# Second parts of the weights: a subtraction on GpSimd, or a DMA that adds the weights from DRAM

## The chip, the cores and the metric

The kernel runs on one core of one Trainium2 chip. A core has five engines that run side by side: TensorE (PE in the profile, with its weight loads as PEld), VectorE (DVE), ScalarE (ACT), GpSimd (POOL) and SyncE (SP, which here only issues DMAs). They work on tiles in SBUF; PE writes to PSUM banks. Sixteen DMA engines move data between DRAM and SBUF, for whichever engine issues the DMA. The metric is the device time of one execution in microseconds (us), the median of several runs.

## What is computed

Two transformer-like blocks in float32 over one sequence of 512 tokens of width 1024. Cut to what matters here:

```python
x = layer_norm(x)
h = x @ w_in + b_in                                    # heads of two attentions
mix = concat(swa_sink_attention(h), dsa_attention(h)) @ w_o + b_o
x = layer_norm(ALPHA * x + mix)
x = layer_norm(ALPHA * x + memory_cross_attention(x))  # xa_wq, xa_wk, xa_wv, xa_wo
x = layer_norm(ALPHA * x + square(relu(x @ w_up + b_up)) @ w_down + b_down)
h = x + ssd_mixer(rms_norm(x))                         # ssm_in, chunked scan, ssm_out
h = h + mla_mixer(rms_norm(h))                         # mla_in, latent attention, mla_out
return rms_norm(h)
```

Nearly all of the arithmetic is in the products with the weight matrices.

## The kernel before

Every product is made of three matmuls in the type float32r, which keeps fewer bits than float32. Each float32 operand is split in a first part H (its value rounded to float32r) and a second part L (what the rounding left over), and `mm3` (lines 127 to 131) adds H·H, L·H and H·L into one PSUM bank: a line for each, L129, L130 and L131.

`wload` (L115) does this for the weights. It loads a tile of up to 128 x 1024 float32 (512 KB) with a DMA from SP into `wraw` (3 buffers), ScalarE copies it into `wh` (5 buffers, L121), which rounds it, and GpSimd subtracts `wh` from `wraw` in pieces of 512 columns into `wl` (5 buffers, L124). There are 254 such tiles in the program. For eight of them, those of `xa_wk` at the start, the caller names the engine (`leng`): VectorE for the first, GpSimd for the others. For the other 246 `leng` is None and GpSimd is taken.

The matrix products that use `wload` are written in a few forms. `gemm_s` takes one tile for each 128 output columns and runs 24 matmuls of 512 columns with it (eight slices times three). `gemm_m` takes two slices of 512 columns of a tile for each group of tokens (w_down, xa_wv). `gemm_q` (w_o, xa_wo, ssm_out, mla_out) takes two or four tiles together and goes through the tokens with them, with matmuls of 256 columns; its last group always has four tiles and is gone through four times, once for each 128 tokens. The tile framework orders the instructions of each engine beforehand by its own estimate of when each could run, so the order that stands in the program on one engine depends on what the others are given. Each engine then executes its own list in order and waits at a semaphore where it must. A buffer of `wh` or `wl` is written anew when PE is done with its last matmul, one of `wraw` when both readers are done.

GpSimd also has other work in its list: the products with 1/den in the softmax (L653, L798, L878), the sums and gates of the state space mixer (L1015, L1018, L1055, L1066, L1067, and L95 for a power), and splits of a few activations (L146, L153).

Of the kernel before, what the change touches and what calls it, by code (L numbers as in the profile page):

```python
# [10 lines left out]
ALU = mybir.AluOpType  # L11
# [9 lines left out]
def f32(ap):  # L21
    return ap.bitcast(F32)


class Net:
# [89 lines left out]
    def wload(self, ap, n=1024, shape=None, leng=None):  # L115
        nc = self.nc
        raw = self.wp.tile([P, 1024], F32, tag="wraw", name=self.nm("wraw"), bufs=3)
        h = self.wp.tile([P, 1024], F32R, tag="wh", name=self.nm("wh"), bufs=5)
        l = self.wp.tile([P, 1024], F32R, tag="wl", name=self.nm("wl"), bufs=5)
        nc.sync.dma_start(raw[:, :n], ap)  # L120
        nc.scalar.activation(h[:, :n], raw[:, :n], AF.Copy)  # L121
        for o in range(0, n, 512):
            e = slice(o, min(n, o + 512))
            (leng or nc.gpsimd).tensor_tensor(l[:, e], raw[:, e], f32(h[:, e]), op=ALU.subtract)  # L124
        return h, l

    def mm3(self, out, aH, aL, bH, bL, first, last):
# [1496 lines left out]
```

## Time and profile before

| | us |
|---|---|
| median of 3 runs (1727.59 to 1733.44) | 1730.55 |
| profiled execution, its own time | 1732.23 |
| span of the profile | 1730.5 |
| PE busy | 1663.9 (96%) |
| DVE busy | 927.3 (54%) |
| POOL busy | 907.9 (52%) |
| ACT busy | 834.1 (48%) |

Busy time is the time in which an instruction of that engine ran; shares are of the span. The rest of the execution's own time (1.7 us) lies outside the span. A wait is put down to the instruction whose semaphore ended it. Matmuls overlap in PE, so a matmul's duration is longer than the distance to the next, and a PE that is shown as busy may still have small gaps.

### The profile page before, as it was taken

What the parts mean: (1) busy time and instruction counts of PE and PEld (TensorE: products, weight loads), DVE (VectorE), ACT (ScalarE), POOL (GpSimd) and SP (SyncE); (2) the same over time, 40 slices, a digit from 0 to 9 for tenths busy, and PEclk for the clock granted to TensorE, in tenths of its full rate; (3) what the DMA queues carried; (4) which work ended last, traced back from release to release, by engine and by line L of the source; (5) the groups of instructions that cost most, each with busy time, mean ns of one, the idle gap of its engine ahead of it and who ended that gap; (6) DMA issues with size and microseconds to landing.
All of it is one profiled execution on the core that took longest, in us unless ns stands there. A gap on an engine that the chain in (4) does not pass through costs nothing.

```text
span 1730.5 us, 27236 instructions
## 1 busy us (share of the span) xinstructions
PE 1663.9 (96%) x10203; PEld 1479.8 (86%) x10203; DVE 927.3 (54%) x1981; ACT 834.1 (48%) x1694; POOL 907.9 (52%) x833
## 2 busy tenths in 40 slices
PE   6999999999999999999999899998999999999998
PEld 6877889889988888887978788888999888989898
DVE  7579763742653014303778877779321306667522
ACT  4455663453443123313557767767433326565532
POOL 6746434353375445544558777777634544344431
PEclk9999999999999999999999999999999999999999
DMA  7634313232232222222332222332324332122341
GB/s 282 196 107 130 106 48 143 95 110 86 86 120 87 97 99 88 95 98 95 125 117 92 86 86 98 110 101 95 146 98 155 130 123 76 52 75 92 110 141 50
DMA packets 68181, 187.23 MB, mean 108 GB/s; under 512 B 9968, under 2 KB 16544, under 8 KB 67792
## 3 DMA queue, kind: packets, MB, share of 16 engines
q1 hardware_dynamic: 50128, 152.95, 26.0%
q10 hardware_dynamic: 17632, 30.43, 5.5%
q8 instruction: 80, 1.31, 0.3%
q0 software_dynamic: 288, 2.10, 0.3%
q14 instruction: 53, 0.43, 0.1%
HBM read 163.86 MB, written 14.78 MB: 103 GB/s over the span
## 4 chain that ended last, share of the span: by engine, by line
PE 71%; DVE 14%; ACT 5%; issue 4%; DMA 3%; POOL 3%; ACTq 0%; DVEq 0%; SPq 0%; POOLq 0%
PE mm L129 12%; PE mm L131 12%; PE mm L130 12%; PE acc L129 5%; PE acc L130 5%; PE acc L131 5%; PE sc L130 2%; PE sc L131 2%; PE sc L129 2%; DMA Dm<-acd 2%; DVE xbc L948 2%; POOL wl L124 2%; PE pv L130 2%; PE pv L131 1%; PE pv L129 1%
## 5 line engine op out<-in xcount | busy, mean ns | idle before, releaser
L124 POOL TENSOR_TENSOR wl<-wraw,wh 128x512 fp32r<-128x512 f32 (+1 forms) x498 | 665.3, 1360 | 515.5 <-ACT wh L121 492.7
L121 ACT ACTIVATE wh<-wraw 128x1024 fp32r<-128x1024 f32 (+4 forms) x254 | 258.3, 1019 | 404.0 <-PE acc L131 123.7
L129 PE MATMUL mm<-xaH,wh 128*128 128x512 f32 x552 | 221.3, 401 | 1.8 <-DVE qbL L140 1.1
L131 PE MATMUL mm<-xaH,wl 128*128 128x512 f32 x552 | 220.8, 400 | 0.0
L130 PE MATMUL mm<-xaL,wh 128*128 128x512 f32 x552 | 220.5, 399 | 0.0
L129 PE MATMUL mm<-wh,xaH 128*128 128x256 f32 x512 | 145.1, 284 | 1.4 <-ACT xaH L145 1.4
L131 PE MATMUL mm<-wh,xaL 128*128 128x256 f32 x512 | 144.6, 284 | 0.9 <-DVE xaL L143 0.9
L130 PE MATMUL mm<-wl,xaH 128*128 128x256 f32 x512 | 144.2, 282 | 0.0
L129 PEld LDWEIGHTS mm<-xaH,wh 128*128 128x128 f32 x552 | 104.9, 190 | 26.1 <-DVE qbL L140 1.5
L131 PEld LDWEIGHTS mm<-xaH,wl 128*128 128x128 f32 x552 | 104.8, 190 | 24.5
L130 PEld LDWEIGHTS mm<-xaL,wh 128*128 128x128 f32 x552 | 104.9, 190 | 23.9
L878 POOL TENSOR_SCALAR S<-S,den 128x128 f32<-128x128 f32 (+1 forms) x96 | 50.9, 534 | 103.2 <-DVE den L877 88.2
L129 PEld LDWEIGHTS mm<-wh,xaH 128*128 128x128 f32 x512 | 96.4, 188 | 2.0 <-ACT xaH L145 1.8
L131 PEld LDWEIGHTS mm<-wh,xaL 128*128 128x128 f32 x512 | 96.2, 188 | 1.2 <-DVE xaL L143 1.1
L131 PE MATMUL mm<-wh,xbL 128*128 128x256 f32 x336 | 94.5, 284 | 2.4 <-DVE xbL L143 2.3
L130 PEld LDWEIGHTS mm<-wl,xaH 128*128 128x128 f32 x512 | 96.4, 188 | 0.2
L129 PE MATMUL mm<-wh,xbH 128*128 128x256 f32 x336 | 95.4, 285 | 0.7 <-DVE lnsum L256 0.5
L130 PE MATMUL mm<-wl,xbH 128*128 128x256 f32 x336 | 94.4, 282 | 0.0
L698 DVE TENSOR_TENSOR rl<-rl 128x512 f32<-128x512 f32 x32 | 43.7, 1365 | 78.5 <-ACT rl L697 78.5
L948 DVE SCALAR_TENSOR_TENSOR xbc<-mm,conv_w,xbc 128x511 f32<-128x511 f32 (+2 forms) x84 | 62.2, 742 | 18.2 <-ACT xbc L946 17.3
L131 PEld LDWEIGHTS mm<-wh,xbL 128*128 128x128 f32 x336 | 63.0, 189 | 3.5 <-DVE xbL L143 2.9
L876 ACT ACTIVATE S<-S,mx 128x128 f32<-128x128 f32 (+1 forms) x96 | 53.7, 560 | 22.6 <-DVE mx L875 20.8
(631 smaller groups left out, 4782.3 us busy)
## 6 DMA issues: line engine op xcount, KB each, us to landing
wraw<-in_w_up SPq DMA_DIRECT2D x32, 512.0 KB, 3.2
wraw<-in_w_down SPq DMA_DIRECT2D x32, 512.0 KB, 3.2
wraw<-in_ssm_xbc SPq DMA_DIRECT2D x32, 512.0 KB, 3.2
Dm<-acd ACTq DMA_DIRECT2D x32, 256.0 KB, 3.3
wraw<-in_ssm_out SPq DMA_DIRECT2D x16, 512.0 KB, 3.5
wraw<-in_mla_z SPq DMA_DIRECT2D x16, 512.0 KB, 3.4
wraw<-in_mla_out SPq DMA_DIRECT2D x16, 512.0 KB, 3.5
wraw<-in_ssm_z SPq DMA_DIRECT2D x14, 512.0 KB, 3.3
```

The source lines that it names most:

```text
L121: nc.scalar.activation(h[:, :n], raw[:, :n], AF.Copy)
L124: (leng or nc.gpsimd).tensor_tensor(l[:, e], raw[:, e], f32(h[:, e]), op=ALU.subtract)
L129: mm(out, aH, bH, start=first, stop=False, skip_group_check=True)
L130: mm(out, aH, bL, start=False, stop=False, skip_group_check=True)
L131: mm(out, aL, bH, start=False, stop=last, skip_group_check=True)
L698: nc.vector.tensor_tensor(r, r, r, op=ALU.mult)
L876: nc.scalar.activation(s, s, AF.Exp, bias=mx, scale=-1.0, accum_out=den)
L878: nc.gpsimd.tensor_scalar(s, s, den, 1.0, op0=ALU.mult, op1=ALU.mult)
L948: nc.vector.scalar_tensor_tensor(o[:, j:], ps[:, :T - j], cw[:, m, 3 - j:4 - j], o[:, j:], op0=ALU.mult, op1=ALU.add)
```

## The change

In `wload`, where no engine is named, the subtraction is replaced. GpSimd writes the negated weights into `wl`, in one instruction over the whole tile; the write rounds to float32r, so `wl` then holds the negated first part. Then GpSimd issues a DMA that reads the same weights from DRAM a second time and adds them onto `wl`. When it has landed, `wl` holds weights minus first part, as before. GpSimd no longer reads `wh`.

```diff
@@ -119,9 +119,14 @@
         l = self.wp.tile([P, 1024], F32R, tag="wl", name=self.nm("wl"), bufs=5)
         nc.sync.dma_start(raw[:, :n], ap)
         nc.scalar.activation(h[:, :n], raw[:, :n], AF.Copy)
+        if leng is None:
+
+            nc.gpsimd.tensor_scalar(l[:, :n], raw[:, :n], -1.0, 1.0, op0=ALU.mult, op1=ALU.mult)
+            nc.gpsimd.dma_start(l[:, :n], ap, accum_op=ALU.add)
+            return h, l
         for o in range(0, n, 512):
             e = slice(o, min(n, o + 512))
-            (leng or nc.gpsimd).tensor_tensor(l[:, e], raw[:, e], f32(h[:, e]), op=ALU.subtract)
+            leng.tensor_tensor(l[:, e], raw[:, e], f32(h[:, e]), op=ALU.subtract)
         return h, l
```

Lines behind it stand five lower: the three matmuls of `mm3` are L134, L135 and L136 in the changed kernel.

In GpSimd's list, at the first tiles that the change touches (`win_m`, three tiles of 984, 984 and 656 columns, right behind the last tile of `xa_wk`), there stood:

```order
L124 TENSOR_TENSOR wl_597<-wraw_595,wh_596 128x512
L124 TENSOR_TENSOR wl_597<-wraw_595,wh_596 128x472
L124 TENSOR_TENSOR wl_640<-wraw_638,wh_639 128x512
L124 TENSOR_TENSOR wl_640<-wraw_638,wh_639 128x472
L124 TENSOR_TENSOR wl_683<-wraw_681,wh_682 128x512
```

And now:

```order
L124 TENSOR_SCALAR wl_597<-wraw_595 128x984
L124 TENSOR_SCALAR wl_640<-wraw_638 128x984
L125 DMA wl_597<-in_win_m 128x984
L125 DMA wl_640<-in_win_m 128x984
L124 TENSOR_SCALAR wl_683<-wraw_681 128x656
```

The DMA of a tile stands behind its own negation, and here behind the negation of the next tile too. In the long products the two simply take turns, a negation and its DMA for each tile.

PE's list is moved where the framework expects the second parts later than before. In the product with `w_o`, at the first matmul that reads `wl_3465` (third tile of the last group; the tiles `tr`, `sc` and `mm` are PSUM banks of different tokens), there stood:

```order
L130 MATMUL sc_3398<-wl_3342,xaH_2342 128x256
L131 MATMUL sc_3398<-wh_3341,xaL_2343 128x256
L131 MATMUL tr_3477<-wh_3457,xaL_2343 128x256
L129 MATMUL tr_3477<-wh_3464,xaH_2342 128x256
L130 MATMUL tr_3477<-wl_3465,xaH_2342 128x256
L131 MATMUL tr_3477<-wh_3464,xaL_2343 128x256
```

And now, first where the tile's first part is taken, and after the line of "..." where its second part is:

```order
L135 MATMUL sc_3398<-wl_3342,xaH_2342 128x256
L136 MATMUL sc_3398<-wh_3341,xaL_2343 128x256
L136 MATMUL tr_3477<-wh_3457,xaL_2343 128x256
L134 MATMUL tr_3477<-wh_3464,xaH_2342 128x256
L134 MATMUL mm_3541<-wh_3450,xaH_2342 128x256
...
L134 MATMUL mm_3605<-wh_3464,xaH_2342 128x256
L135 MATMUL tr_3477<-wl_3465,xaH_2342 128x256
L136 MATMUL tr_3477<-wh_3464,xaL_2343 128x256
```

The matmuls themselves are the same; the first one with `wl_3465` stands 52 places further down PE's list, behind work for the next tokens with tiles that are there already. In the long products with `w_up`, `w_down` and `mla_z` PE's list is as it was.

## Rows read from the trace of the kernel before

**Rows 1.** Page, part 1: busy us (share) xinstructions of each engine.

```profile
PE 1663.9 (96%) x10203; PEld 1479.8 (86%) x10203; DVE 927.3 (54%) x1981; ACT 834.1 (48%) x1694; POOL 907.9 (52%) x833
```

**Rows 2.** Waits, whole execution: engine, line <- releaser: us in total, times, longest.

```profile
POOL wl L124 <- ACT wh L121: 492.7, 158, 17.1
...
PE px L1078 <- ACT y L1073: 5.8, 5, 2.0
...
PE acc L131 <- POOL wl L124: 0.2, 1, 0.2
```

**Rows 3.** Windows: busy us (xinstructions) of each engine, PE clock, DMA share, GB/s.

```profile
47.00:88.00 41.00, 41.00 (x220) 35.31 (x219) 21.89 (x55) 20.40 (x40) 31.05 (x26) 1.00 0.64 200
...
550.00:600.00 50.00, 50.00 (x215) 40.21 (x214) 3.77 (x5) 8.79 (x9) 20.77 (x17) 1.00 0.28 95
850.00:1200.00 350.00, 330.18 (x2068) 291.61 (x2067) 279.90 (x435) 243.31 (x525) 252.97 (x217) 0.99 0.31 101
```

**Rows 4.** Timeline of ACT in the w_down product: start, us, instruction, idle before.

```profile
563.36 1.06 ACT L121 ACTIVATE wh<-wraw 128x1024 fp32r<-128x1024 f32 x1 [4.54 <-PE acc L131]
569.03 1.06 ACT L121 ACTIVATE wh<-wraw 128x1024 fp32r<-128x1024 f32 x1 [4.62 <-PE acc L131]
```

**Rows 5.** Timeline of POOL in the same stretch.

```profile
564.49 2.54 POOL L124 TENSOR_TENSOR wl<-wraw,wh 128x512 fp32r<-128x512 f32 x2 [3.06 <-ACT wh L121]
```

**Rows 6.** POOL's groups, shapes apart: busy us, mean ns of one, idle before.

```profile
L124 POOL TENSOR_TENSOR wl<-wraw,wh 128x512 fp32r<-128x512 f32 x469 | 643.8, 1395 | 515.5 <-ACT wh L121 492.7 <-issue 11.8 <-PE acc L279 4.0
...
L111 POOL TENSOR_SCALAR ln_g<-ln_g 128x1024 f32<-128x1024 f32 x3 | 3.1, 1049 | 23.1 <-DMA ln_g<-in_ln_g 23.1
```

**Rows 7.** Line L501: POOL's only DMAs (1 MB each, SBUF to SBUF).

```profile
L501 POOL DMA_DIRECT2D xaH<-iqH x1: 794/794/794, 208.3 to 208.3; - x1
L501 POOL DMA_DIRECT2D xaL<-iqL x1: 538/538/538, 209.1 to 209.1; - x1
...
DMA to landing us min/median/max: 4.7/5.5/6.4
```

**Rows 8.** Line L120, the loads of wraw from SP.

```profile
DMA to landing us min/median/max: 2.3/3.3/6.6
```

**Rows 9.** Page, part 3: DMA queue, kind: packets, MB, share of 16 engines.

```profile
q1 hardware_dynamic: 50128, 152.95, 26.0%
...
q0 software_dynamic: 288, 2.10, 0.3%
```

**Rows 10.** Timeline of POOL from 45.7 us: the first two tiles of win_m.

```profile
45.55 5.84 POOL L124 TENSOR_TENSOR wl<-wraw,wh 128x512 fp32r<-128x512 f32 x4
```

**Rows 11.** Timeline of PE: first matmul with the second part of win_m.

```profile
49.70 0.32 PE L130 MATMUL acc<-wl,xaH 128*128 128x328 f32 x1
```

**Rows 12.** Timeline of POOL: last group of w_o, tiles two and three.

```profile
284.84 2.53 POOL L124 TENSOR_TENSOR wl<-wraw,wh 128x512 fp32r<-128x512 f32 x2 [11.44 <-ACT wh L121]
...
291.87 2.52 POOL L124 TENSOR_TENSOR wl<-wraw,wh 128x512 fp32r<-128x512 f32 x2 [4.50 <-ACT wh L121]
```

**Rows 13.** Timeline of PE: the first matmuls with those two second parts.

```profile
289.12 0.28 PE L130 MATMUL tr<-wl,xaH 128*128 128x256 f32 x1
...
295.67 0.28 PE L129 MATMUL tr<-wh,xaH 128*128 128x256 f32 x1
295.79 0.28 PE L130 MATMUL tr<-wl,xaH 128*128 128x256 f32 x1
```

**Rows 14.** Groups of POOL and of DVE from 850 to 1200 us, the state space mixer.

```profile
L124 POOL TENSOR_TENSOR wl<-wraw,wh 128x512 fp32r<-128x512 f32 x93 | 129.9, 1419 | 34.4 <-ACT wh L121 32.0 <-issue 2.4
...
L1032 DVE TENSOR_TENSOR Dm<-Dm,cbm 128x512 f32<-128x512 f32 x32 | 37.1, 1185 | 6.3 <-ACT Dm L1031 6.1
```

**Rows 15.** Waits from 850 to 1200 us.

```profile
ACT Dm L1030 <- DMA Dm<-acd: 20.2, 15, 2.6
...
ACT y L1073 <- POOL gss L95: 8.9, 11, 2.5
```

**Rows 16.** Timeline of POOL from 84 us, the xa_wv product.

```profile
87.69 2.52 POOL L124 TENSOR_TENSOR wl<-wraw,wh 128x512 fp32r<-128x512 f32 x2 [2.99 <-ACT wh L121]
```

## The prediction

> **What bounds the kernel now.** I read the busy times first: PE 1663.9 of 1730.5 us, the others at half of the span [rows 1]. So PE bounds, and an edit off PE counts only where PE has to wait. The waits come next. GpSimd's largest is for ScalarE's `wh` (492.7 us), while PE's wait for `wl` in an accumulator product is 0.2 us in total [rows 2]. That is a producer that stands before full buffers. The windows and the timeline show it in a long product: 215 matmuls of 512 columns in 50 us with PE busy throughout [rows 3], so 0.233 us each and 5.6 us for the 24 matmuls of a tile; ScalarE starts a copy every 5.67 us, each time when PE has freed a buffer [rows 4], and GpSimd follows at once [rows 5].
>
> From the freed buffer to the finished second part it takes 564.49 + 2.54 - 563.36 = 3.67 us [rows 4, 5]. With five buffers, the tile is then used about 4 x 5.6 - 3.7 = 18.7 us later. This lead is the cover of everything that the change adds to the making of a tile.
>
> **The change, part by part.** It touches 246 of the 254 tiles.
>
> *GpSimd's time.* Removed: two subtractions, 2.54 us undisturbed [rows 5], 2 x 1.395 = 2.8 us on average [rows 6]. Added: a negation of 128 x 1024, for which I take the same operation on the same shape in L111, 1.05 us [rows 6], and the issue of a DMA, 0.54 to 0.79 us [rows 7]. GpSimd gets back about 1.0 us a tile. In the long products this is worth nothing, since GpSimd waits there anyway.
>
> *ScalarE.* The second part no longer waits for `wh`. Both wait for PE's buffers, so this is in the next term and gives nothing more.
>
> *Time from the freed buffer to the finished second part.* Now: negation 1.05, 0.1 for the semaphore, and L, the time from issue to landing. No accumulating DMA is in the trace. The nearest rows are a plain load of the same 512 KB, median 3.3 us [rows 8], and GpSimd's own DMAs of 1 MB, 4.7 and 6.4 us [rows 7]. An accumulation of 512 KB reads 512 KB twice, so I take the 1 MB that lay alone, 4.7. It makes 5.85 us, 2.2 more than before; the bounds are 0.8 and 3.9 more. Where the lead is 18.7 us this costs nothing, and if the cover were gone, it would cost these 2.2 us once for each restart of the ring, not per tile. Three kinds of places have a shorter lead:
> - The start, at `win_m`. GpSimd subtracts two tiles from 45.55 us on, the first done near 48.0 [rows 10]; PE takes it at 49.70 [rows 11]. In the new order the first DMA stands behind two negations: issue at 45.55 + 2.1 = 47.65, landing at 52.35 (50.95 to 54.05). PE's list puts three more matmuls ahead, about 0.4 us. Late by 2.25 us (0.85 to 3.95). Behind PE, everything of this product stands still, so this is a full loss.
> - The last group of `w_o`. The second tile was done at 284.84 + 2.53 = 287.37 and used at 289.12, a lead of 1.75; the third 294.39 and 295.79, a lead of 1.4 [rows 12, 13]. The third (and the fourth, alike) gets 52 matmuls of 0.12 us ahead of it [rows 13], 6.2 us, and is safe. The second stays: late by 2.2 - 1.75 = 0.45 us (0 to 2.15).
> - The last groups of `xa_wo`, `ssm_out` and `mla_out`. A tile of the group before comes free each 24 x 0.12 = 2.9 us, the new ones are wanted each 1.44 us; the fourth has 2.9 + 3 x 1.44 - 3.67 = 3.5 us. 0 (to 0.4 each, 1.2 together).
>
> *The DMA engines.* A tile's load costs them 0.26 x 1730.5 / 152.95 x 0.524 = 1.54 us, a copy of this size within SBUF 0.003 x 1730.5 / 2.10 x 0.524 = 1.3 us [rows 9]. The addition reads both: between 1.54 (second read hidden) and 2.84 us; I take 2.84. In a long product the engines are busy 0.28 x 5.6 = 1.6 us a tile [rows 3] and would be 4.4 of 5.6: no cost. From 47 to 88 us they are busy 26 of 41 us, and about eight tiles make it 49, which is 8 us too many. There the tiles are made ahead of their use, and at 87.69 GpSimd waits for freed buffers again [rows 16]; I take 0, with 4 us as the far end.
>
> *The state space mixer.* From 850 to 1200 us PE lacks 350 - 330.2 = 19.8 us, and GpSimd is busy 253 of 350 [rows 3]. 46 tiles at 2.84 [rows 14] free some 46 us of it. The way by which GpSimd holds up PE goes over `gss` and `y`: ScalarE waits 8.9 us for `gss` [rows 15], PE 5.8 us for `y` [rows 2]. I take 2 of these 5.8 us as gained (0 to 5.8). Against it, the DMA share there rises from 0.31 by 46 x 2.84 / 350 = 0.37, and ScalarE waits for `Dm` from a DMA in 15 places, 20.2 us [rows 15]; I take 1 us (0 to 3).
>
> Sum: 2.25 + 0.45 + 0 + 0 - 2 + 1 = +1.7 us, from -5 to +14. On the profiled execution's 1732.23 that is 1734; the median of the runs shown is 1.7 us lower, so a run should be near 1733. A measurement of this kernel can tell about 0.3% (5.2 us) from no change: the forecast is no change.
>
> **The rivals.**
> *The addition lands later than any row here.* The issue is an instruction of GpSimd's own [rows 7]. If each one stood behind one VectorE instruction (1.2 us, [rows 14]) and L were 6.4, a tile would be done 5.1 us later than before: 5.2 at `win_m`, 3.35 at `w_o`, 3 x 1.6 at the last groups, and with the mixer's -1 some +12 us, 1744; each further microsecond of L adds about 5. For it: the two issues in the trace differ by half, 0.79 and 0.54 us [rows 7]. Against it: in the long products VectorE is busy 3.8 of 50 us [rows 3]. The Trainium skill, "SBUF — State Buffer", section "SBUF: two separate sides", says that VectorE in its two-port modes locks GpSimd out of the port through which it writes descriptors, and gives 620 ns alone against 3100 ns beside a copy. By that 2.5 us in place of 1.2, an estimate is 5 x 1.3 = 6.5 us above the 1744; the trace's two issues show nothing of this size, and no run here shows it for an accumulation.
>
> *The DMA engines become the bound.* It decides from 5.6 - 1.6 = 4.0 us a tile on. The rows reach 2.84; if the addition costs twice that, 5.7, a tile takes 7.3 us instead of 5.6. About 165 tiles have 24 or 48 matmuls that take 5.6 us (w_up 32, w_down 32, ssm_xbc 32, ssm_out, mla_z and mla_out 16 each, win_s 13, xa_wq 8), so 165 x 1.65 = 270 us: 2000. At 4.5 us a tile it would be about 1810. For it: nothing in the trace adds in a DMA, so the price has no row of its own. Against it: both reads together stay well below.
>
> *Faster.* With a GpSimd that reads one input once where it read two twice, the mixer's chains over GpSimd and VectorE shorten by more than I take: all 5.8 us of PE's wait for `y` and a third of the other 14 us, and the start loses less: -9 us, 1723. For it: VectorE is busy 280 of 350 us there [rows 3]. Against it: most of PE's short waits there name VectorE or ScalarE.
>
> **Chances.** No change 0.38 (1727 to 1737); late landing, slower by 6 to 30 us, 0.27; DMA engines as the bound 0.15; faster 0.20. So faster by over 0.3% 0.20, within 0.3% 0.38, slower 0.42. The likeliest is 1733. The range of 8 in 10 leaves out the DMA bound and a little at either end: 1720 to 1770.
>
> **What the changed profile would show.** GpSimd's busy time falls by about 200 us, with 246 negations of about 1.05 us. The DMAs of the new line land in 4 to 6.5 us, and the DMA share in a long product is near 0.8 or less. PE's list of waits has a new entry of 1 to 4 us near 50 us and little else; the matmuls of the long products keep 0.233 us. The forecast is wrong if the DMA share reaches 1 in the w_up product or PE's matmuls there come in groups with gaps (DMA bound); if issues on GpSimd take over 1.5 us or landings over 8 (late landing); or if the mixer gives back more than 6 us (faster).

## The result and the profile after

The changed kernel takes 1802.6 us (median of four runs, 1800.6 to 1808.0) where the kernel before took 1730.6 beside it: ratio 1.042, interval 1.0405 to 1.0436. It is 72 us slower. I had forecast 1733, from 1720 to 1770: wrong. The profiled execution has a span of 1806.2 us. Lines from L123 on stand five lower than before: L124 is the negation, L125 the accumulating DMA.

Page of the changed kernel, part 1, as [rows 1]:

```profile
PE 1690.9 (94%) x10203; PEld 1504.6 (83%) x10203; DVE 846.0 (47%) x1981; ACT 831.2 (46%) x1694; POOL 736.0 (41%) x841
```

GpSimd has 172 us back, and PE is *busy* 27.0 us longer for the same 10203 matmuls, at a mean granted clock of 0.970 instead of 0.987. So of the span's 75.7 us more, some two thirds are time in which PE stands and one third is slower matmuls. The windows of the changed kernel, in columns as [rows 3]:

```profile
49.00:97.00 48.00, 42.19 (x204) 35.78 (x202) 18.95 (x55) 19.31 (x38) 23.92 (x25) 0.93 1.04 268
...
300.00:350.00 50.00, 36.27 (x261) 34.20 (x260) 26.28 (x64) 16.88 (x26) 15.68 (x15) 0.88 0.88 245
550.00:600.00 50.00, 50.00 (x215) 40.24 (x214) 6.43 (x10) 15.00 (x18) 17.03 (x19) 1.00 0.87 188
```

The long products lose nothing: 215 matmuls in 50 us, with the transfer engines at 0.87 instead of 0.28. In the other two windows (`win_m`; the last group of `w_o` and what follows) PE stands, the granted clock is below 1 and the transfer engines are nearly full. How much of that is the accumulation's, only the experiments tell.

Timeline of GpSimd in the w_up product, as [rows 5]:

```profile
699.76 1.04 POOL L124 TENSOR_SCALAR wl<-wraw 128x1024 fp32r<-128x1024 f32 x1 [3.40 <-PE mm L136]
701.10 0.89 POOL L125 DMA_DIRECT2D wl<-in_w_up  x1 [0.30 <-POOL wl L124]
```

GpSimd still waits for PE's buffers. The groups of GpSimd, the page's queues (part 3, as [rows 9]), and the issues (ns, min/median/max) and landing of the new DMAs (line L125) and the landing of the raw loads (line L120, as [rows 8]):

```profile
L124 POOL TENSOR_SCALAR wl<-wraw 128x1024 fp32r<-128x1024 f32 (+4 forms) x246 | 265.8, 1085 | 573.3 <-PE mm L136 191.2 <-PE mm L135 130.6 <-PE acc L135 123.0
...
L125 POOL DMA_DIRECT2D wl<-in_w_up x32 | 28.9, 914 | 9.0 <-POOL wl L124 9.0
```

```profile
q0 software_dynamic: 35712, 125.09, 37.4%
q1 hardware_dynamic: 50128, 152.95, 26.4%
```

```profile
L125 POOL DMA_DIRECT2D wl<-in_w_up x32: 877/887/1232, 447.9 to 723.6; - x32
...
L125 POOL DMA_DIRECT2D wl<-in_win_s x13: 870/897/1554, 54.9 to 159.0; - x13
...
DMA to landing us min/median/max: 4.5/8.0/14.5
```

```profile
DMA to landing us min/median/max: 2.6/5.9/13.9
```

A tile's accumulation costs the engines 0.374 x 1806.2 / 125.09 x 0.524 = 2.83 us; I had taken 2.84. (This is the time of its packets. Shares above 1, as from 49 to 97 us, show that packets of one engine overlap in this count.) But it lands after 8.0 us in the median, not 4.7, and a raw load after 5.9 instead of 3.3. PE meets this at the start of `win_m` (timeline of PE, as [rows 11]) with the 1.77 us of the last line; the 4.04 us ahead of them are a wait for ScalarE, which comes from the new order, as order_after below shows. Other waits of PE, and one of ScalarE in the mixer (waits, as [rows 15], whole execution):

```profile
49.40 0.71 PE L134 MATMUL acc<-wh,xaH 128*128 128x328 f32 x3
54.14 0.42 PE L134 MATMUL acc<-wh,xaH 128*128 128x328 f32 x1 [4.04 <-ACT xaH L150]
56.33 0.64 PE L135 MATMUL acc<-wl,xaH 128*128 128x328 f32 x1 [1.77 <-DMA wl<-in_win_m]
```

```profile
PE mm L135 <- DMA wl<-in_ssm_out: 7.5, 2, 5.5
PE tr L135 <- DMA wl<-in_w_o: 4.2, 2, 2.4
```

```profile
ACT Dm L1035 <- DMA Dm<-acd: 61.7, 23, 6.9
```

The direct waits for `wl` come to little over 20 us in all; the rest needs experiments.

### The profile page after: what moved, and what is told of

It reads as the page before. It is cut to its first block, busy times and chain, and to the rows that moved or that the text cites. A ratio compares the mean times of both kernels' runs of the same rounds, so it can differ in the third digit from the quotient of the medians.

```text
span 1806.2 us, 27200 instructions
## 1 busy us (share of the span) xinstructions
PE 1690.9 (94%) x10203; PEld 1504.6 (83%) x10203; DVE 846.0 (47%) x1981; ACT 831.2 (46%) x1694; POOL 736.0 (41%) x841
## 3 DMA queue, kind: packets, MB, share of 16 engines
q0 software_dynamic: 35712, 125.09, 37.4%
## 5 line engine op out<-in xcount | busy, mean ns | idle before, releaser
L124 POOL TENSOR_SCALAR wl<-wraw 128x1024 fp32r<-128x1024 f32 (+4 forms) x246 | 265.8, 1085 | 573.3 <-PE mm L136 191.2
L136 PE MATMUL mm<-xaH,wl 128*128 128x512 f32 x552 | 221.3, 402 | 2.8 <-DMA wl<-in_win_s 2.8
L134 PE MATMUL mm<-xaH,wh 128*128 128x512 f32 x552 | 221.9, 402 | 0.4 <-ACT wh L121 0.4
L135 PE MATMUL mm<-xaL,wh 128*128 128x512 f32 x552 | 221.3, 401 | 0.0
L134 PE MATMUL mm<-wh,xaH 128*128 128x256 f32 x512 | 147.8, 289 | 1.4 <-ACT xaH L150 1.4
L135 PE MATMUL mm<-wl,xaH 128*128 128x256 f32 x512 | 147.7, 289 | 0.0
L136 PE MATMUL mm<-wh,xaL 128*128 128x256 f32 x512 | 146.6, 288 | 0.0
L136 PEld LDWEIGHTS mm<-xaH,wl 128*128 128x128 f32 x552 | 105.3, 191 | 27.7 <-DMA wl<-in_win_s 3.2
L134 PEld LDWEIGHTS mm<-xaH,wh 128*128 128x128 f32 x552 | 105.4, 191 | 25.0 <-ACT wh L121 0.8
L135 PEld LDWEIGHTS mm<-xaL,wh 128*128 128x128 f32 x552 | 105.4, 191 | 24.0
L135 PE MATMUL mm<-wl,xbH 128*128 128x256 f32 x336 | 97.0, 290 | 8.7 <-DMA wl<-in_ssm_out 7.5
L134 PEld LDWEIGHTS mm<-wh,xaH 128*128 128x128 f32 x512 | 99.9, 195 | 2.1 <-ACT xaH L150 1.8
L134 PE MATMUL mm<-wh,xbH 128*128 128x256 f32 x336 | 96.6, 289 | 3.3 <-ACT xbH L150 2.8
L135 PEld LDWEIGHTS mm<-wl,xaH 128*128 128x128 f32 x512 | 99.4, 194 | 0.2
L136 PEld LDWEIGHTS mm<-wh,xaL 128*128 128x128 f32 x512 | 99.3, 194 | 0.1
L136 PE MATMUL mm<-wh,xbL 128*128 128x256 f32 x336 | 96.1, 289 | 0.0
L703 DVE TENSOR_TENSOR rl<-rl 128x512 f32<-128x512 f32 x32 | 22.8, 713 | 110.3 <-ACT rl L702 110.3
L135 PEld LDWEIGHTS mm<-wl,xbH 128*128 128x128 f32 x336 | 65.2, 194 | 9.4 <-DMA wl<-in_ssm_out 7.9
L1035 ACT ACTIVATE Dm<-Dm,acum 128x128 f32<-128x128 f32 x128 | 41.7, 390 | 61.7 <-DMA Dm<-acd 61.7
```

What stands on the lines that cost most here:

```text
L124: nc.gpsimd.tensor_scalar(l[:, :n], raw[:, :n], -1.0, 1.0, op0=ALU.mult, op1=ALU.mult)
L134: mm(out, aH, bH, start=first, stop=False, skip_group_check=True)
L135: mm(out, aH, bL, start=False, stop=False, skip_group_check=True)
L136: mm(out, aL, bH, start=False, stop=last, skip_group_check=True)
L703: nc.vector.tensor_tensor(r, r, r, op=ALU.mult)
L1035: nc.scalar.activation(Dm[:, h, :], Dm[:, h, :], AF.Relu, bias=acum[:, c, 4 * g + h:4 * g + h + 1], scale=-1.0)
```

## The experiments

There are two theories. *Late finish*: a second part is complete some 5 us later than by subtraction, and PE pays wherever it has caught up. *Shared engines*: the traffic makes other transfers late, and PE waits for those. A third came from the order of the instructions, which the scheduler changed too.

**The order, apart from the arithmetic.** Four engines (PE, ScalarE, VectorE, SyncE) are tied to a recorded order by edges that order issue and wait for nothing; GpSimd's order stays free.

```
+    for e, code in ORDER.items():
+        rows, k, prev = traced[e], -1, None
+        for step in zlib.decompress(base64.b85decode(code)).decode().split(","):
+            k += int(step) + 1
+            if prev is not None:
+                tc.add_manual_dep(rows[k], prev.name, info, reason="pin")
+            prev = rows[k]
```

The recorded lists (`ORDER`) and the lines around are left out here. Order_before is the changed arithmetic in the old order, order_after the old arithmetic in the new one.

> The changed arithmetic (negation and accumulating DMA for the same 246 tiles), but TensorE, ScalarE, VectorE and SyncE are made to issue their instructions in the order of the kernel before; only GpSimd's order is left free. Late finish theory (a second part is finished 5 to 8 us later than by subtraction, and TensorE pays this wherever it has caught up with the loads): 1790 to 1830 us, since the lateness stays. Shared transfer engines theory (the 125 MB of accumulation slow the raw loads and the small copies): also 1790 to 1830. Order theory (the new instruction order, not the DMA, costs the time): 1727 to 1740.

> The arithmetic of the kernel before (GpSimd subtraction, no accumulating DMA), but TensorE, ScalarE, VectorE and SyncE issue in the order of the changed kernel. Late finish theory and shared transfer engines theory: 1725 to 1745 us, near the kernel before. Order theory: 1790 to 1810, near the changed kernel. In between, each theory has its share of the 72 us.

Measured: order_before 1806.3 us (1.0431, 1.041 to 1.0452), order_after 1769.8 (1.022, 1.0201 to 1.0238). So the accumulation costs 74 us in the order made for a subtraction, and 33 in the new one (1802.6 against 1769.8). The new order costs 37 us if the arithmetic is the old one, and with the new arithmetic it saves next to nothing (1802.6 against 1806.3). The accumulation alone is enough for the whole loss, but the two don't add up, and in the changed kernel itself the order has a large part early on. The first load for `w_up` (line L120, the time after the comma) in the kernel before, the changed kernel, order_before and order_after, and then `win_m` in order_after (timeline of PE):

```profile
L120 SPq DMA_DIRECT2D wraw<-in_w_up x32: 327/328/328, 402.7 to 685.2; - x32
L120 SPq DMA_DIRECT2D wraw<-in_w_up x32: 327/328/328, 423.0 to 706.4; - x32
L120 SPq DMA_DIRECT2D wraw<-in_w_up x32: 327/328/328, 428.1 to 710.7; - x32
L120 SPq DMA_DIRECT2D wraw<-in_w_up x32: 327/328/328, 419.6 to 702.9; - x32
```

```profile
53.66 0.42 PE L129 MATMUL acc<-wh,xaH 128*128 128x328 f32 x1 [4.20 <-ACT xaH L145]
```

The changed kernel is 20.3 us late there, and the new order alone, without any accumulation, 16.9. Of the 5.8 us that PE stands from 49 to 97 us in the changed kernel, 4 are a wait for ScalarE that order_after has too. So what follows explains the 74 us of the accumulation in the old order; how the changed kernel's own 72 divide from place to place was not measured.

From here on every kernel is tied to the old order, except the next two. What the tying costs by itself was not measured; quarter_sub below, tied and with the old arithmetic in smaller pieces, is at 0.9987.

**Which tiles.** An accumulation for some tensors, subtraction for the rest:

```
+        if leng is None and ap.tensor.name in ("in_w_up", "in_w_down", "in_mla_z"):
+            nc.gpsimd.tensor_scalar(l[:, :n], raw[:, :n], -1.0, 1.0, op0=ALU.mult, op1=ALU.mult)
+            nc.gpsimd.dma_start(l[:, :n], ap, accum_op=ALU.add)
+            return h, l
```

These lines stand ahead of the old subtractions, which do the other tiles. Long_only is this, short_only its complement, first_only and mixer_only other lists.

> Accumulating DMA only in the 80 tiles of w_up, w_down and mla_z, subtraction in the other 166. Late finish theory: 1727 to 1736 us, no change, because there every tile is asked for 10 us or more after its load. Shared transfer engines theory: 1731 to 1736 too, since the engines are busy for 4.4 us of the 5.6 that a tile's products take. If the dense products do pay, 1740 to 1760.

> The complement: subtraction in w_up, w_down and mla_z, accumulating DMA in the other 166 tiles. Late finish theory and shared transfer engines theory: 1795 to 1808 us, nearly all of the loss of the changed kernel. If the long products carried a share of the loss, 1760 to 1790.

> Accumulating DMA only in the tiles ahead of the feed forward part (win_m, win_s, xa_wv, w_uk, w_uv, w_o, xa_wq, xa_wo), subtraction elsewhere, order of the kernel before. By the same run: +28 us by the start of w_up, so 1755 to 1762, of which win_m 9 and the last group of w_o 14.

> Order of the kernel before; accumulating DMA only in the tiles of ssm_xbc, ssm_z and ssm_z0 (the state space mixer), subtraction elsewhere. By the run in the order of before, which lost some 30 us between 830 and 1221 us of the kernel before: 1755 to 1765. If the mixer's loss was only carried in by what had gone before: 1731 to 1740.

Measured: long_only 1731.3 (1.000, 0.9988 to 1.0012), short_only 1804.7 (1.043, 1.0396 to 1.0464), first_only 1760.2 (1.0169, 1.0153 to 1.0186), mixer_only 1761.9 (1.0176, 1.0152 to 1.02). Of the 74 us, 30 lie ahead of the feed forward part, 31 in the mixer, none in the long products; the other 13 (`ssm_out` and the MLA part) are the difference. The traces of the kernel before and of order_before can be compared matmul by matmul, since PE's list is the same: order_before is 28 us late where the kernel before is at 400 us, 58 at 1221, 70 at 1330 and 76 at the end. In this execution 11 us are lost in `ssm_out` and 6 in `mla_out`.

The first 30 are lost at `win_m` and, for the most part, at the last group of `w_o`. In order_before, `win_m` (timeline of PE), then `w_o`: timeline of GpSimd, then of PE, then windows:

```profile
56.50 0.64 PE L135 MATMUL acc<-wl,xaH 128*128 128x328 f32 x1 [6.88 <-DMA wl<-in_win_m]
```

```profile
300.33 1.05 POOL L124 TENSOR_SCALAR wl<-wraw 128x1024 fp32r<-128x1024 f32 x1 [10.27 <-PE sc L135]
301.68 0.88 POOL L125 DMA_DIRECT2D wl<-in_w_o  x1 [0.30 <-POOL wl L124]
```

```profile
309.76 0.58 PE L135 MATMUL tr<-wl,xaH 128*128 128x256 f32 x1 [3.78 <-DMA wl<-in_w_o]
...
325.14 0.58 PE L135 MATMUL tr<-wl,xaH 128*128 128x256 f32 x1 [5.48 <-DMA wl<-in_w_o]
```

```profile
290.00:300.00 10.00, 10.00 (x80) 9.74 (x80) 2.18 (x4) 1.86 (x4) 0.06 (x1) 1.00 0.01 2
300.00:310.00 10.00, 6.22 (x48) 5.88 (x47) 0.69 (x1) 1.66 (x2) 1.93 (x2) 0.90 0.73 216
310.00:320.00 10.00, 8.46 (x39) 7.44 (x39) 2.91 (x12) 3.04 (x4) 3.50 (x4) 0.59 0.84 272
320.00:330.00 10.00, 4.86 (x28) 4.86 (x29) 0.80 (x6) 0.53 (x1) 3.23 (x4) 0.66 1.04 275
330.00:340.00 10.00, 10.00 (x85) 10.00 (x85) 5.55 (x15) 4.36 (x7) 0.00 (x0) 1.00 0.12 25
```

One DMA is issued at 301.68, and PE takes its tile at 309.76, 8.1 us later, having stood for 3.78. Then the granted clock is 0.59 in the window, a mix of the two levels 1.2 and 2.4 GHz. Matmuls of the same 256 columns ahead of the stall and behind it (timeline of PE):

```profile
299.00 0.28 PE L136 MATMUL sc<-wh,xaL 128*128 128x256 f32 x1
299.12 0.28 PE L134 MATMUL sc<-wh,xaH 128*128 128x256 f32 x1
...
311.21 0.41 PE L135 MATMUL tr<-wl,xaH 128*128 128x256 f32 x1
311.42 0.41 PE L136 MATMUL tr<-wh,xaL 128*128 128x256 f32 x1
```

They follow each other after 0.12 us ahead of it and after 0.21 behind it. This stall is paid twice: once standing, once in the slow matmuls that come next. Not every stall is: in the changed kernel PE stands for 2.44 us at the same place (at 304.84), and the granted clock stays at 1.00 (windows of the changed kernel):

```profile
300.00:310.00 10.00, 6.17 (x44) 5.40 (x43) 1.38 (x2) 2.14 (x3) 1.92 (x2) 1.00 0.97 299
310.00:320.00 10.00, 8.28 (x69) 8.07 (x69) 2.85 (x16) 2.02 (x2) 4.87 (x5) 1.00 0.99 316
```

**What in the accumulation.** In the old order: neg_pin leaves out the DMA, eighth_pin accumulates 128 of 1024 columns (its edit is shown), plain_pin writes all the weights in place of adding them. In none of them is the second part the right one.

```
-            nc.gpsimd.dma_start(l[:, :n], ap, accum_op=ALU.add)
+            nc.gpsimd.dma_start(l[:, :128], ap[:, :128], accum_op=ALU.add)
```

> Order of the kernel before on TensorE, ScalarE, VectorE and SyncE; the second part is only the negation, the accumulating DMA is left out (so the addition of the weights is not computed). All that is left of the change is GpSimd's saving of 1.5 to 1.8 us a tile. Late finish and shared engines theories: 1720 to 1735 us, no slower than before. If GpSimd's new rows themselves (negation at full width ahead of other work) delay something: above 1740.

> The same, but with an accumulating DMA on the first 128 of a tile's 1024 columns (the other 7/8 of the addition are left out): one issue and one landing for each tile, 64 KB in place of 512. Shared engines theory: 1725 to 1740 us, the traffic is gone. Late finish theory, if most of the landing is a fixed time from issue to completion: 1750 to 1790; if the landing grows with the bytes: 1730 to 1745. The landing itself shows which: under 4 us or over 6.

> The same, with the full 512 KB, but the DMA on GpSimd's queue writes the weights in place of adding them (the second part is then the weights themselves). Reads and writes of DRAM and SBUF are as for a load; only the add is gone. If the accumulation itself is what makes the transfer slow: landing 4 to 5 us in place of 8, 1.5 us of engine time a tile in place of 2.8, and 1745 to 1765 us. If the way through GpSimd's queue is: landing 7 to 8 us and 1790 to 1810.

Measured: neg_pin 1693.1 (0.9791, 0.977 to 0.9812), eighth_pin 1719.9 (0.994, 0.9918 to 0.9963), plain_pin 1726.0 (0.9973, 0.9961 to 0.9985). I had not expected the first: with the addition left out, the change gains 38 us. Of line L125, the landing in eighth_pin, then in plain_pin, then in order_before, and the queue of plain_pin:

```profile
DMA to landing us min/median/max: 2.6/3.8/9.3
```

```profile
DMA to landing us min/median/max: 3.2/4.9/10.0
```

```profile
DMA to landing us min/median/max: 4.6/7.9/14.3
```

```profile
q0 software_dynamic: 35712, 125.09, 21.9%
```

This is a ladder: no DMA -38 us; landing 3.8 us, -11; 4.9 us, -5; 7.9 us, +74. The plain DMA costs the engines 0.219 x 1727.8 / 125.09 x 0.524 = 1.59 us a tile, the accumulation 2.83. A plain transfer of the same bytes over the same queue leaves the kernel about where it was, by a gain of 38 us and a loss of 33; with the add in it the kernel is 80 us slower than that.

The Trainium skill, "DMA: Bandwidth & Descriptors", section "Anatomy of one DMA — SWDGE (gpsimd) path", fits such a DMA by 2.0 us plus its bytes over 436 thousand a microsecond, an estimate of 3.2 us for 512 KB. Among the loads here the plain DMA is slower: its full tiles of `ssm_xbc` land after 3.6 us at least and 4.8 in the median (the 3.2 in the row above is a tile of 256 KB). The accumulation's 5.3 and 7.7 for the same tiles, in order_before, are far from the fit.

**Traffic that nobody waits for.** Four kernels issue from GpSimd, for each tile, a DMA that no engine waits for: traffic_pin a copy of 512 KB from DRAM to DRAM behind the old subtractions, the others, behind the negation, a copy of 64 KB (neg_issue_pin), a copy of 1 MB (neg_traffic_pin), or a store of the tile to DRAM in pieces of 1 KB (neg_store_pin).

> The arithmetic and order of the kernel before, with an added DMA on GpSimd behind each pair of subtractions that copies the same 512 KB from DRAM to DRAM into a buffer that nobody reads: the traffic of the accumulation and its issue time on GpSimd, and nobody waits for it. Late finish theory: 1730 to 1750 us. Shared engines theory (raw loads and small copies land later): 1780 to 1810.

> Order of the kernel before; negation, and behind each an unrelated 64 KB copy from DRAM to DRAM issued by GpSimd that nobody waits for (the addition is left out). Against the negation alone (1693 us) it adds GpSimd's issue time only. Late finish theory: 1696 to 1712 us, the rest of the 27 us that the eighth of an accumulation cost being its landing. If the issue time alone is the price: 1715 to 1722.

> The same with a copy of 1 MB in place of 64 KB (the tile read twice and written to DRAM twice), to put on the transfer engines the 2.5 to 2.8 us a tile that the accumulation took; nobody waits for it. Shared engines theory: raw loads land 3 us later, the mixer's Dm copies make ScalarE wait 60 us in place of 25, and the time is 1760 to 1800. Late finish theory: within 15 us of the run with 64 KB, 1700 to 1725.

> Order of the kernel before; negation (the addition is left out), and behind it on GpSimd's queue a DMA that stores the finished tile to DRAM in pieces of 1 KB, which nobody waits for. GpSimd has the negation, the wait for it and one issue, as in the changed kernel; the transfer engines get an estimated 2 to 2.8 us a tile (worked out from the 62 ns a packet of the eighth's 512 bytes and the 170 ns a packet of the plain 4 KB). Late finish theory: 1700 to 1715 us, near the 1705 of the 64 KB copies. Shared engines theory: raw loads land at 6 us or later and the time is 1750 to 1800, near the changed kernel in the order of before.

Measured: traffic_pin 1790.8 (1.0342, 1.0305 to 1.0378), neg_issue_pin 1705.0 (0.9848, 0.9832 to 0.9865), neg_traffic_pin 2506.7 (1.4471, 1.4395 to 1.4548), neg_store_pin 1714.1 (0.99, 0.9881 to 0.9919). Two of these don't answer the question. In neg_traffic_pin the raw loads landed after 20 us, with these copies taking a quarter of the engines' time, so they held up the loads as no accumulation did (its loads in the page's part 6):

```profile
wraw<-in_w_up SPq DMA_DIRECT2D x32, 512.0 KB, 21.3
```

In traffic_pin GpSimd has the full subtraction *and* an issue, and is busy 1008 us; whether its loss is GpSimd's time or the traffic it can't tell, since ScalarE's wait for `Dm` is longer there too (38.6 us against 20.2). Neg_store_pin is the fair one: negation, wait, issue, traffic, and nobody waits. Its queue and its raw loads:

```profile
q0 software_dynamic: 130176, 125.09, 28.5%
```

```profile
DMA to landing us min/median/max: 2.5/4.2/9.6
```

That is 2.04 us a tile, for 9 us more than the 64 KB copies and 92 us under order_before. So unawaited traffic of 2 us a tile costs little, at least in this direction. It is short of the 2.83, though, and the raw loads land sooner (4.2 us against 6.6 in order_before), so the 92 us aren't split by it.

For the part ahead of `w_up` something can be said. The first load for `w_up` in eighth_pin, plain_pin and neg_store_pin (402.7 in the kernel before, 428.1 in order_before):

```profile
L120 SPq DMA_DIRECT2D wraw<-in_w_up x32: 327/328/328, 408.0 to 688.4; - x32
L120 SPq DMA_DIRECT2D wraw<-in_w_up x32: 327/328/328, 407.8 to 687.9; - x32
L121 SPq DMA_DIRECT2D wraw<-in_w_up x32: 327/328/328, 396.3 to 676.6; - x32
```

Eighth_pin moves an eighth of the bytes and is 12 us later than neg_store_pin. So about 12 us there come from waiting for a landing at all, with hardly any traffic; the 20 more of order_before come with the full add, and whether by its longer landing or by its load on the engines stays open.

**The mixer.** In mixer_only, ScalarE's wait for the copies of `Dm` is three times that of [rows 15], while these copies take 3.7 us in the median where they took 3.3 before. It is the longest that grew, from 4.0 to 7.8:

```profile
ACT Dm L1034 <- DMA Dm<-acd: 63.2, 22, 8.3
```

```profile
DMA to landing us min/median/max: 3.0/3.7/7.8
```

So both kernels were run without them:

```
-            nc.scalar.dma_start(Dm, acd[c * 32 + 4 * g:c * 32 + 4 * g + 4, :].partition_broadcast(P))
...
-                nc.scalar.activation(Dm[:, h, :], Dm[:, h, :], AF.Relu, bias=acum[:, c, 4 * g + h:4 * g + h + 1], scale=-1.0)
+                nc.scalar.activation(Dm[:, h, :], self.ident, AF.Relu, bias=acum[:, c, 4 * g + h:4 * g + h + 1], scale=-1.0)
```

> The kernel before in its own order, without the 32 Dm copies of the mixer (ScalarE's decay rows are computed from a constant tile that is always there, so the decays are not the reference's). It is the base for the next run. ScalarE waited 20 us for these copies in the kernel before: 1705 to 1731 us.

> The same without Dm copies, with the accumulating DMA in the mixer's tiles alone (as in mixer_only, which was 31 us above the kernel before). If the delayed Dm copies are what the mixer loses: within 10 us of nodm_sub. If the late second parts, or GpSimd's wait and issue, are: 25 to 35 us above it. If nodm_acc is under nodm_sub, GpSimd's saving shows once the Dm copies don't stand in the way.

Measured: nodm_sub 1717.0 (0.9917, 0.9901 to 0.9932), nodm_acc 1716.3 (0.991, 0.9897 to 0.9924). Without the copies, accumulating in the mixer costs nothing net: PE still waits 6.4 us there for `wl` (nodm_acc), and gains as much elsewhere. So the mixer's net 31 us go through `Dm`. That the traffic makes these copies late fits their longest landing, in the old order: 4.0 us before, 4.4 in eighth_pin, 5.5 to 6.1 in plain_pin, neg_store_pin and traffic_pin, 7.7 in order_before. So there the shared engines theory fits, and late second parts cost no more than the rest of the change gives back.

**Versions that should gain.**

```
-        for o in range(0, n, 512):
-            e = slice(o, min(n, o + 512))
+        step = 512 if leng is not None else 1024
+        for o in range(0, n, step):
+            e = slice(o, min(n, o + step))
```

> The arithmetic and the order of the kernel before, with one GpSimd subtraction of 1024 columns in place of two of 512. The negation alone gained 38 us by saving GpSimd 1.6 us a tile; if the two subtractions carry 0.2 us or so of fixed time, some 5 us are to be had: 1723 to 1729. If their time goes by columns alone: 1728 to 1733.

> The arithmetic and order of the kernel before with four GpSimd subtractions of 256 columns in place of two of 512. One of 1024 took 2.46 us where two of 512 took 2.72, and cost 15 us: what counted was that the first half is ready 1.1 us earlier. If so, quarters give the first columns 0.6 us earlier still but hold GpSimd some 0.5 us longer a tile (estimated from the 0.26 us between one and two): 1725 to 1740 us. If GpSimd's longer time decides in the mixer: 1738 to 1750.

> The kernel before in its own order, but 23 of the 32 Dm copies are issued one to four rows earlier on ScalarE (never within two rows of the row that gives their buffer free). If ScalarE's wait for them is what holds TensorE in the mixer: its wait falls from 20 us to under 12 and the time to 1720 to 1728. If the earlier issue only makes ScalarE wait for the buffer instead: 1728 to 1738, with VectorE named as what ended the wait.

Measured: one_sub 1747.3 (1.0095, 1.0077 to 1.0113), quarter_sub (step 256) 1729.2 (0.9987, 0.9975 to 0.9999), early_dm 1737.1 (1.005, 1.0034 to 1.0066). The edit shown is one_sub's. One subtraction of 1024 saves GpSimd 2 x 1.395 - 2.46 = 0.33 us a tile and loses 15 us; the first half ready early is worth more than the time, as I read it, for PE can begin with it. This is not shown, and there is a rival: GpSimd's instruction holds up VectorE. VectorE is busy for 927.3 us in the kernel before, 970.5 in one_sub, 891.9 in quarter_sub and 837.4 in neg_pin. One of its products, the same 32 instructions, in the kernel before, one_sub and neg_pin (groups of DVE):

```profile
L698 DVE TENSOR_TENSOR rl<-rl 128x512 f32<-128x512 f32 x32 | 43.7, 1365 | 78.5 <-ACT rl L697 78.5
L699 DVE TENSOR_TENSOR rl<-rl 128x512 f32<-128x512 f32 x32 | 75.1, 2351 | 56.9 <-ACT rl L698 56.9
L702 DVE TENSOR_TENSOR rl<-rl 128x512 f32<-128x512 f32 x32 | 23.8, 745 | 108.1 <-ACT rl L701 108.1
```

With no instruction of GpSimd on a weight tile beside it, as 28 of the 32 in neg_pin, it takes 0.69 us. In one_sub, 30 of the 32 end 0.55 us after the subtraction that runs beside them, whenever they began. Which of the two readings the 15 us come from, no run tells. Quarters are no more than the measurement can tell. Early_dm brought ScalarE's wait from 20.2 to 16.8 us, and yet the whole is 6 us longer; I did not trace where. No version here that leaves nothing out beats the kernel before by 0.3%.

## Why the prediction was wrong

**What bounds the kernel: right.** PE bounds, and the lead of 18.7 us covers all in the long products: long_only is 1.000, and the transfer engines' 4.4 us of 5.6 cost nothing there.

**The time from issue to landing: the step that failed first.** I took L = 4.7 us from "the 1 MB that lay alone", with 6.4 as the far end. The median is 8.0, past both ends; the shortest, 4.5, is a smaller tile, and no full tile of `ssm_xbc` landed before 5.1. The engines' price (2.83) was right, to the second digit by luck, since the 0.3% from which I had its 1.3 has only one. But I let the transfer lie alone. A tile's accumulation flies beside other tiles' loads: a load lands after 5.9 us instead of 3.3, the accumulation after 8.0, and what it would take alone no run shows. Its price was wrong as well. I wrote that "each further microsecond of L adds about 5"; from plain_pin to order_before, 3.0 us of landing cost 80, some 27 for each, with the engines' higher load in it. Nor does plain_pin, with a landing of 4.9 us and 0.9973 inside my "no change", save the rest of the sum: there a gain of 38 and a loss of 33 nearly cancel, where I had a gain of 2 and losses of 3.7.

**The short leads, and the order.** `win_m`: late by 2.25 us forecast. In the changed kernel PE waits 1.77 us for the accumulation, behind 4.04 for ScalarE that the new order brings; in the old order it is 6.9 in a single wait, and there also the raw loads were late. `w_o`: 0.45 forecast; 2.44 + 1.72 measured in the changed kernel, 3.78 + 5.48 in the old order. I had called its third and fourth tile safe because the new order put 52 matmuls ahead; the 1.72 (like the 5.48) is the third tile's all the same, issued at 308.19 and taken at 319.50. And the new order, which I counted as a help, costs 37 us by itself under the old arithmetic: a term that I put at nothing without a reason. The clock was in no term of the sum either; PE's 27 us more go with the lower granted clock, 0.970 in the mean.

**The DMA engines in the first part.** "I take 0, with 4 us as the far end": the window from 49 to 97 us has the engines at 1.04 and PE standing for 5.8 us. These are the 4.04 and the 1.77 from above, so no stall there is the engines' alone. All terms ahead of the feed forward part together were 2.7; first_only, in the old order, measured 30.

**The mixer: right in kind and far off in both sizes.** The gain from GpSimd's time was set at 2 us "of these 5.8". The negation alone gains 38 us over the whole kernel and 26 with a 64 KB issue; `gss` and `y` are not the only ways on which GpSimd's time lies, and VectorE's busy time falls with it, from 927 to 837 us. The collision with the `Dm` copies was set at 1 us (0 to 3); it is 31 net, and without the copies nothing of it is left. I read the median landing of such copies; the longest ones set the wait.

**The rivals.** *Late landing* had the mechanism and not its way: no issue is held for long (0.89 us in `w_up`, 1.55 the longest of all, in `win_s`), and nothing here shows the 3100 ns that the Trainium skill, "SBUF — State Buffer", section "SBUF: two separate sides", gives for a DMA beside a copy. By its own terms the measured landing would have given 1744 + 1.6 x 5 = 1752, some 50 us short. *DMA engines as the bound* is refuted in the long products by its own mark, the share of 0.87. *Faster* is what happens without the addition, and by more than that rival said (38 us, not 9).

**Open.** How some 20 of the first part's 30 us divide between the accumulation's longer landing and its load on the engines. Why the new order costs 37 us under the old arithmetic. Through which waits the negation's 38 us are gained. What an accumulation with less traffic beside it would land in.

## What to carry to other kernels

Price a DMA put in place of an engine's instruction by its landing among the transfers that run beside it, not by a row in which it lay alone, and put that landing against the lead at each start of a product, one by one; a ring of buffers hides it in long products only. Then look for every other transfer with a short lead (here 256 KB copies that one engine waits for in line), and read its longest landing. To tell arithmetic from a scheduler's new order, tie the order and change one at a time; the two parts need not add up.

## What the hardware showed beyond this

- An accumulating DMA from DRAM onto SBUF took 0.374 x 1806.2 x 16 / 35712 = 0.303 us of an engine for each packet, the plain one with the same packets 0.219 x 1727.8 x 16 / 35712 = 0.170. Its issue held GpSimd for 0.89 us, the plain one's 0.58 (`w_up`); ahead of it GpSimd waited 0.30 us for its own negation.
- The same subtractions, loads and matmuls in another order differ by 37 us.
- A negation of 128 x 1024 on GpSimd takes 1.04 us in `w_up`, a subtraction of the same tile 2.46 in one and 2.79 in two (means).
- An instruction of VectorE (`rl`, 128 x 512) that takes 0.69 us alone took 2.35 in the mean beside GpSimd's subtractions of 1024 columns, and 1.37 beside those of 512.
